# A two-block transformer kernel: two of five gate-and-up chunks per feed-forward as seven block products

## The chip, the cores and the metric

The kernel runs on one core of a Trainium2 chip. The metric is the device time of one execution in microseconds (us); the kernel before takes 1632.77 us, the median of three runs. Names of engines are those of the profile: PE is TensorE (matmuls; PEld are its weight loads), DVE is VectorE, ACT is ScalarE, POOL is GpSimd, SP is SyncE, whose queue issues the DMAs.

## The reference, cut to what matters

256 rows of 1024 elements pass through two blocks, all in float32. Block 1 has two gated feed-forwards, a mixer and a gated side input. Block 2 has four feed-forwards (called s0 to s3 below), a gated linear attention between s0 and s1 and a retention between s2 and s3, each followed by a layer norm. The four feed-forwards are:

```python
def swiglu_2(x, w_in, w_out):            # x 256x1024, w_in 1024x5632, w_out 2816x1024
    gate, up = jnp.split(x @ w_in, 2, axis=-1)
    return (jax.nn.silu(gate) * up) @ w_out
...
        h = layer_norm(DN_ALPHA * h + 0.5 * swiglu_2(h, ffn_w_in[i, 0], ffn_w_out[i, 0]), ln_g[i, 0], ln_b[i, 0])
```

## The kernel before, in words

**Units.** Weights come from memory in units of 128x2048 float32 (1 MB each). A unit is half of the 1024-deep contraction (four blocks of 128 rows) for 512 columns. `fetch` (lines 145 to 163) loads one into a `raw` tile by an SP DMA, rounds it on ACT to `whi` (line 159) and lets DVE write what is left over, `wlo = raw - whi` (line 162). There are 4 `raw` tiles and 5 each of `whi` and `wlo`. Activations, transposed, are split in the same manner (`split`, lines 193 to 200). So each float32 block product is three matmuls of 128x512 (`mm3`, lines 179 to 183: hi·hi, hi·lo, lo·hi).

**A feed-forward** (`ffn`, lines 344 to 399). The 256 rows are two tiles, t = 0 and 1. The 2816 hidden columns are five chunks (c = 0 to 4) of 512 columns of gate and of up, and a last one of 256 and 256. A chunk has four units: gate lower half, gate upper half, up lower half, up upper half. For each t and each of gate and up the PE adds 8 blocks into one PSUM tile (`mm`, 5 of them), which makes 2 x 2 x 8 x 3 = 96 matmuls a chunk. `finish` (line 348) then takes silu of gate on ACT (`sg`, line 352) and multiplies by up on DVE (`pr`, line 353). `turn` transposes both `pr` tiles on PE (4 + 4 transposes of 128x128, line 190) and splits them into `hT`, input of the down product (`lagged`, lines 304 to 342, 11 units).

**What sets the order.** The code is written in one sequence. `unit` (line 165) hands out the next unit of the plan (`all_units`, line 68) and fetches further ones ahead; `defer` and `tick` put steps such as transposes some matmuls later. A scheduler then gives every engine its own order; on the chip every queue goes in order, and semaphores join them. At the end of a layer `ln_post` (line 264) writes y, and `turn_in` (line 249) transposes it for the next one.

Of the kernel before, what the change touches and what calls it, by code (L numbers as in the profile page):

```python
# [11 lines left out]
F32 = mybir.dt.float32  # L12
F32R = mybir.dt.float32r
# [6 lines left out]
P = 128  # L20
# [29 lines left out]

def ffn_units(g, u, d):

    out = []
    for c in range(5):
        out += [(g, 2 * c), (g, 2 * c + 1), (u, 2 * c), (u, 2 * c + 1)]
    return out + [(g, 10), (g, 11)] + [(d, i) for i in range(11)]
# [4 lines left out]


MIX_ORDER = [1, 0, 2, 3, 4, 5, 6, 7]
GLA_ORDER = [1, 0, 2, 4, 3, 5]
# [15 lines left out]

class Build:
# [6 lines left out]
    def open(self, ctx):  # L88
        def pool(name, space=None):
# [55 lines left out]
    def fetch(self, fine=False, begun=None):  # L145

        nc = self.nc
        name, i = self.plan[len(self.ready)]
        raw = begun or self.T("raw", [P, UNIT], F32)
        hi = self.T("whi", [P, UNIT], F32R)  # L150
        lo = self.T("wlo", [P, UNIT], F32R)
        parts = 4 if fine else 1
        n = UNIT // parts
        for j in range(parts):
            s = slice(j * n, (j + 1) * n)
            if begun is None or j:
# [57 lines left out]
    def sumsq(self, srcs, scale):  # L214

        st = self.small(len(srcs), "ss")
        for i, s in enumerate(srcs):
            jk = self.T("jk", [P, CW], F32)
            self.nc.scalar.activation(jk[:, :s.shape[-1]], s, AF.Square, scale=scale, accum_out=st[:, i:i + 1])  # L219
        return st  # L220
# [27 lines left out]

    def turn_in(self, xT, t, n, u):

        self.defer(TURN[t] + n, lambda: xT.__setitem__(n, self.splitT(u)))

# [10 lines left out]

    def ln_post(self, t, acc, g, b, half, last=False):

# [15 lines left out]
        for n in range(2):  # L281
            sl = slice(n * CW, (n + 1) * CW)
            y = self.T("y", [P, CW], F32)
            nc.vector.scalar_tensor_tensor(out=y, in0=h[:, sl], scalar=r, in1=b[:, sl], op0=ALU.mult, op1=ALU.add)  # L284
            if last:
                nc.sync.dma_start(out=self.out[t * P:(t + 1) * P, sl], in_=y)
            else:
                self.turn_in(xT, t, n, y)
                self.nc.gpsimd.tensor_scalar(out=h[:, sl], in0=y, scalar1=ALPHA, scalar2=0.0, op0=ALU.mult, op1=ALU.add)
# [3 lines left out]
    def proj(self, ps, x, w, n=CW, kb=4, k0=0, nk=None):  # L293


        nk = nk or kb * len(w)
        for i in range(kb * len(w)):
            k = k0 + i
            self.settle(lambda: x[k // 4] is not None)
            self.mm3(ps[:, :n], x[k // 4][:, k % 4, :], w[i // kb][:, i % kb, :n], k == 0, k == nk - 1)  # L300
            if i % 2:
                self.tick()

    def lagged(self, x, name, n_units, after, lag=LAG, have=None, extra=None):
# [38 lines left out]

    def ffn(self, xT, r, wg, wu, wd, after, first=False):
        nc = self.nc
        hT = {}

        def finish(c, t, ps_g, ps_u, n):
# [41 lines left out]
        for t in range(0 if first else 1, NT):  # L390
            finish(0, t, pss[t, wg], pss[t, wu], CW)
        for c in range(1, 6):
            for nm in (wg, wu) if c < 5 else (wg,):
                w = [self.unit(nm, 2 * c + i, 4) for i in range(2)]
                for t in range(NT):
                    pss[t, nm] = self.M()
                    self.proj(pss[t, nm], xT[t], w)
# [218 lines left out]
    def gla(self, xT, after):  # L616
# [235 lines left out]
    def run(self, ctx):  # L852
# [12 lines left out]
        nc.scalar.activation(warm, self.mhalf[:, :1], AF.Silu)  # L865
        idle = self.T("jk", [P, CW], F32).bitcast(BF16)[:, :CW]
        nc.gpsimd.memset(idle, 0.0)
# [58 lines left out]
        def ln_layer(body, i, half, last):  # L926
            g, b = self.gain("gp", f"ln_g{i}"), self.gain("gq", f"ln_b{i}")
            xT = [None] * NT

            def after(t, acc):  # L930
                xT[t] = self.ln_post(t, acc, g, b, half, last)

# [3 lines left out]
        for i in range(6):  # L936
            if i % 3 != 1:
                f = 2 * (i // 3) + (i % 3) // 2
                body = lambda after: self.ffn(nx, None, f"s{f}g", f"s{f}u", f"s{f}d", after)
# [4 lines left out]
            nx = ln_layer(body, i, i % 3 != 1, i == 5)  # L944

# [110 lines left out]
```

## Time and profile before

| | |
|---|---|
| time, median of 3 runs | 1632.77 us (1632.32 to 1633.8) |
| the profiled execution, its own time | 1633.42 us |
| its span, first to last instruction | 1631.6 us |
| granted PE clock, mean over the span | 0.997 of full speed (2.4 GHz) |
| PE busy | 1619.3 us (99%), 7520 matmul records |
| DVE busy | 932.8 us (57%) |
| ACT busy | 722.3 us (44%) |
| POOL busy | 131.3 us (8%) |
| DMA | 308 MB, mean 189 GB/s |

Busy time is the union of the spans of an engine's instructions. Matmuls overlap each other in the pipeline, so the time that one of them costs is read from the distance between the starts of two that follow each other, not from its own span. The same holds for two DVE or ACT instructions that stand one behind the other. Idle time of an engine costs nothing unless another engine waits at its end.

### The profile page before, as it was taken

Reading aid. Unit: us, or ns where it says so; the run is one execution under the profiler, and the core shown is the slowest. Engines: PE = TensorE matmul, PEld = TensorE weight load, DVE = VectorE, ACT = ScalarE, POOL = GpSimd, SP = SyncE. Lnnn points to the kernel's source line nnn. Section 1 sums busy time; section 2 is a strip of 40 time slices with the busy share of each in tenths; the row PEclk is TensorE's granted clock in tenths of the full one; section 3 lists DMA queues with packets and bytes.
Section 4 is the critical chain, followed back from the end, with each engine's and each line's share of the span. In section 5 each row is a group of like instructions: output and inputs, shape, how many; then the busy total and the mean of one; then the engine's idle time right before and its main releaser. Section 6 shows DMA issues by size and latency. Waiting matters only on the chain. (4 is left out here: it accounts for less than half of the span.)

```text
span 1631.6 us, 18183 instructions
## 1 busy us (share of the span) xinstructions
PE 1619.3 (99%) x7520; PEld 1339.6 (82%) x7520; DVE 932.8 (57%) x818; ACT 722.3 (44%) x715; POOL 131.3 (8%) x138
## 2 busy tenths in 40 slices
PE   9999999999999999999999999999999999999998
PEld 6888888888888888888888888888887888888886
DVE  5644665575543865446747544664538666485444
ACT  6443555444433744433644443444424444344431
POOL 0000200020000300003012000100003300010000
PEclk9999999999999999999999999999999999999999
DMA  9754664545454664545536454555445644464540
GB/s 357 262 189 155 221 218 143 205 175 213 167 194 155 226 227 163 201 155 207 195 135 225 168 200 155 195 219 206 173 162 206 216 155 160 149 238 176 204 146 35
DMA packets 49650, 308.09 MB, mean 189 GB/s; under 512 B 6032, under 2 KB 7056, under 8 KB 14880
## 3 DMA queue, kind: packets, MB, share of 16 engines
q1 hardware_dynamic: 49280, 306.67, 51.6%
q8 instruction: 59, 0.97, 0.2%
q10 hardware_dynamic: 288, 0.27, 0.1%
q14 instruction: 23, 0.19, 0.0%
HBM read 305.86 MB, written 1.05 MB: 188 GB/s over the span
## 5 line engine op out<-in xcount | busy, mean ns | idle before, releaser
L162 DVE TENSOR_TENSOR wlo<-raw,whi 128x2048 fp32r<-128x2048 f32 (+1 forms) x287 | 631.4, 2206 | 480.6 <-ACT whi L159 480.5
L159 ACT CAST whi<-raw 128x2048 fp32r<-128x2048 f32 (+1 forms) x286 | 524.1, 1838 | 554.6 <-PE mm L183 190.2
L181 PE MATMUL mm<-whi,xTh 128*128 128x512 f32 x1296 | 514.0, 397 | 0.0
L183 PE MATMUL mm<-whi,xTl 128*128 128x512 f32 x1296 | 505.8, 390 | 0.4 <-DVE xTl L199 0.4
L182 PE MATMUL mm<-wlo,xTh 128*128 128x512 f32 x1296 | 504.6, 389 | 0.0
L183 PEld LDWEIGHTS mm<-whi,xTl 128*128 128x128 f32 x1296 | 243.2, 188 | 52.9 <-DVE xTl L199 1.2
L181 PEld LDWEIGHTS mm<-whi,xTh 128*128 128x128 f32 x1296 | 243.4, 188 | 49.7 <-issue 1.7
L182 PEld LDWEIGHTS mm<-wlo,xTh 128*128 128x128 f32 x1296 | 243.7, 188 | 48.0
L181 PE MATMUL acc<-whi,hTh 128*128 128x512 f32 x528 | 207.0, 392 | 0.0
L183 PE MATMUL acc<-whi,hTl 128*128 128x512 f32 x528 | 205.7, 389 | 0.0
L182 PE MATMUL acc<-wlo,hTh 128*128 128x512 f32 x528 | 205.5, 389 | 0.0
L183 PEld LDWEIGHTS acc<-whi,hTl 128*128 128x128 f32 x528 | 99.1, 188 | 20.9
L181 PEld LDWEIGHTS acc<-whi,hTh 128*128 128x128 f32 x528 | 99.1, 188 | 20.1
L182 PEld LDWEIGHTS acc<-wlo,hTh 128*128 128x128 f32 x528 | 99.2, 188 | 20.0
L199 DVE TENSOR_TENSOR hTl<-hT,hTh 128x512 fp32r<-128x512 f32 (+1 forms) x72 | 43.7, 642 | 61.0 <-ACT hTh L198 61.0
L276 POOL TENSOR_TENSOR rl<-mv,mhalf 128x1 f32<-128x1 f32 x12 | 11.8, 984 | 762.1 <-DVE mv L275 762.1
L181 PE MATMUL mm<-whi,xh 128*128 128x512 f32 x176 | 69.4, 397 | 1.8 <-ACT xh L884 1.3
L182 PE MATMUL mm<-wlo,xh 128*128 128x512 f32 x176 | 69.2, 393 | 0.2 <-DVE wlo L162 0.2
L183 PE MATMUL mm<-whi,xl 128*128 128x512 f32 x176 | 69.3, 394 | 0.0
L225 POOL TENSOR_TENSOR v<-ss 128x1 f32<-128x1 f32 x16 | 25.1, 1567 | 522.6 <-ACT jk L219 522.6
L352 ACT ACTIVATE sg<-mm 128x512 f32<-128x512 f32 (+1 forms) x48 | 26.9, 560 | 87.3 <-PE mm L183 87.3
L198 ACT CAST hTh<-hT 128x512 fp32r<-128x512 f32 (+1 forms) x72 | 36.6, 554 | 26.3 <-PE hT L190 26.3
(219 smaller groups left out, 1242.4 us busy)
## 6 DMA issues: line engine op xcount, KB each, us to landing
raw<-in_rin SPq DMA_DIRECT2D x24, 1024.0 KB, 4.8
raw<-in_bin SPq DMA_DIRECT2D x16, 1024.0 KB, 5.1
raw<-in_f2g SPq DMA_DIRECT2D x12, 1024.0 KB, 4.8
raw<-in_s0g SPq DMA_DIRECT2D x12, 1024.0 KB, 4.8
raw<-in_gin SPq DMA_DIRECT2D x12, 1024.0 KB, 4.8
raw<-in_s1g SPq DMA_DIRECT2D x12, 1024.0 KB, 4.8
raw<-in_s2g SPq DMA_DIRECT2D x12, 1024.0 KB, 4.8
raw<-in_s3g SPq DMA_DIRECT2D x12, 1024.0 KB, 4.8
```

The source lines that it names most:

```text
L159: nc.scalar.copy(hi[:, s], raw[:, s])
L162: nc.vector.tensor_tensor(out=lo[:, s], in0=raw[:, s], in1=hi[:, s].bitcast(F32), op=ALU.subtract)
L181: mm(ps, x.hi, w.hi, start=start, stop=False)
L182: mm(ps, x.hi, w.lo, start=False, stop=False)
L183: mm(ps, x.lo, w.hi, start=False, stop=stop)
L198: self.nc.scalar.copy(hi, v)
L199: self.nc.vector.tensor_tensor(out=lo, in0=v, in1=hi.bitcast(F32), op=ALU.subtract)
L225: self.nc.gpsimd.tensor_tensor(out=v, in0=st[:, 0:1], in1=st[:, 1:2], op=ALU.add)
L276: nc.gpsimd.tensor_tensor(out=r, in0=mv[:, 1:2], in1=self.mhalf[:, :1], op=ALU.pow)
L352: nc.scalar.activation(sg[:, :n], ps_g[:, :n], AF.Silu)
```

## The change

In each of the four feed-forwards of block 2, chunks 2 and 4 are computed in another way. A chunk is the product of a 2x2 block matrix (row tiles t by halves of the contraction) with a 2x2 block matrix (halves of the contraction by gate and up). Instead of eight block products it is now made of seven, over sums of blocks (`seven`). The weight sums `a+b`, `b+c`, `a+b+c` and `a+b+c+d` are made by DVE in the raw tiles, in place (`fetch_sum`); each of the seven operands is then split into `whi` and `wlo`. The sums of activations (`y`) are made once per feed-forward from copies of the transposed tiles (`turn_in`, `sums_in`). The results are put together by DVE (`seven`). The other chunks now take a unit at a time over both row tiles, in block 1 too. There are 5 `raw` tiles instead of 4; two small tiles change place or type (`jk`, `wg`).

```diff
+SUMS = (("a", None), ("a", "b"), ("b", "c"), ("a", "c"), ("c", None), ("d", None), ("a", "d"))
...
+        four = [(g, 2 * c), (g, 2 * c + 1), (u, 2 * c), (u, 2 * c + 1)]
+        out += [(four, j) for j in range(7)] if c in seven else four
...
+SEVEN = (2, 4)
...
-    BUFS = {"raw": 4, "whi": 5, "wlo": 5, "S": 28, "mm": 5, "tp": 3, "y": 2, "u": 2,
+    BUFS = {"raw": 5, "whi": 5, "wlo": 5, "S": 28, "mm": 5, "tp": 3, "y": 2, "u": 2,
...
+    def fetch_sum(self, four, j):
...
+        for key, at in {0: (("a", 0), ("b", 2)), 2: (("c", 3),), 5: (("d", 1),)}.get(j, ()):
+            r[key] = self.T("raw", [P, UNIT], F32)
+            nc.sync.dma_start(out=r[key], in_=self.ins[four[at][0]][four[at][1]])
+        key, other = SUMS[j]
+        if other:
+            nc.vector.tensor_tensor(out=r[key], in0=r[key], in1=r[other], op=ALU.add)
+        hi, lo = self.T("whi", [P, UNIT], F32R), self.T("wlo", [P, UNIT], F32R)
+        nc.scalar.copy(hi, r[key])
+        nc.vector.tensor_tensor(out=lo, in0=r[key], in1=hi.bitcast(F32), op=ALU.subtract)
+        return Split(hi, lo)
...
+    def sums_in(self, raws):
...
+        sub(r2, r2, raws[1])
+        sub(r4, r4, r2)
...
+            self.nc.scalar.copy(hi, v)
+            self.nc.vector.tensor_tensor(out=lo, in0=v, in1=hi.bitcast(F32), op=ALU.subtract)
...
+    def seven(self, x, y, four, done):
...
+        def times(name, x, j):
+            ps = self.M(name)
+            w = self.unit(four, j, 4, 4)
+            for k in range(4):
+                self.mm3(ps, x[:, k, :], w[:, k, :], k == 0, k == 3)
...
+        nc.scalar.copy(p1, times("P1", x[0][0], 0))
+        p5 = times("P5", y[1], 1)
+        p7 = times("P7", y[3], 2)
+        TT(out=u2, in0=times("P6", y[2], 3), in1=p1, op=ALU.subtract)
+        TT(out=u4, in0=p5, in1=u2, op=ALU.add)
+        TT(out=c22, in0=u4, in1=p7, op=ALU.subtract)
+        TT(out=u2, in0=u2, in1=p7, op=ALU.subtract)
+        TT(out=u4, in0=times("P3", y[4], 4), in1=u4, op=ALU.add)
+        TT(out=p1, in0=times("P2", x[0][1], 5), in1=p1, op=ALU.add)
+        done(0, p1, u4)
+        TT(out=u2, in0=times("P4", x[1][1], 6), in1=u2, op=ALU.subtract)
+        done(1, u2, c22)
...
         for c in range(1, 6):
+            if raws is not None and c == 1:
+                self.defer(4, lambda: y.update(self.sums_in(raws)))
+            if raws is not None and c in SEVEN:
+                self.settle(lambda: y)
+                self.seven(xT, y, [(wg, 2 * c), (wg, 2 * c + 1), (wu, 2 * c), (wu, 2 * c + 1)], finish7(c))
+                continue
             for nm in (wg, wu) if c < 5 else (wg,):
-                w = [self.unit(nm, 2 * c + i, 4) for i in range(2)]
+                for i in range(2):
+                    w = [self.unit(nm, 2 * c + i, 4, 3 if raws is not None else 2)]
+                    for t in range(NT):
+                        if i == 0:
+                            pss[t, nm] = self.M()
+                        self.proj(pss[t, nm], xT[t], w, CW, 4, 4 * i, KD)
```

How it moves the instructions is shown at three places. In the names below, a number behind a tile tells its instances apart, and the L numbers of the changed kernel are those of its own file.

The first is DVE's queue in s0 up to the first seven-product chunk. Of the kernel before, from the last part of one ordinary chunk to the next:

```order
L353 TENSOR_TENSOR pr_4632<-mm_4606,sg_4631 128x512
L162 TENSOR_TENSOR wlo_4746<-raw_4744,whi_4745 128x2048
L353 TENSOR_TENSOR pr_4661<-mm_4635,sg_4660 128x512
L162 TENSOR_TENSOR wlo_4752<-raw_4750,whi_4751 128x2048
L199 TENSOR_TENSOR hTl_4712<-hT_4701,hTh_4711 128x512
L199 TENSOR_TENSOR hTl_4716<-hT_4706,hTh_4715 128x512
L162 TENSOR_TENSOR wlo_4816<-raw_4814,whi_4815 128x2048
L162 TENSOR_TENSOR wlo_4822<-raw_4820,whi_4821 128x2048
```

and of the change, the lead-in to chunk 2 (L186 is the subtraction of a sum's unit, L183 the addition of two raw tiles; the first `wlo` is that of P1, the next that of P5):

```order
L186 TENSOR_TENSOR wlo_4458<-raw_4453,whi_4457 128x2048
L183 TENSOR_TENSOR raw_4453<-raw_4453,raw_4455 128x2048
L223 TENSOR_TENSOR hTl_4432<-hT_4426,hTh_4431 128x512
L304 TENSOR_TENSOR yTl_4442<-y3_4296,yTh_4441 128x512
L183 TENSOR_TENSOR raw_4455<-raw_4455,raw_4516 128x2048
L304 TENSOR_TENSOR yTl_4450<-xr_4169,yTh_4449 128x512
L186 TENSOR_TENSOR wlo_4487<-raw_4453,whi_4486 128x2048
L183 TENSOR_TENSOR raw_4453<-raw_4453,raw_4516 128x2048
```

Where four large subtractions stood in a chunk, there are now additions between them, each ahead of the cast and subtraction of the same tile.

The second is DVE's queue behind chunk 2's last subtraction of a weight sum (the four large rows are units of the ordinary chunk 3):

```order
L168 TENSOR_TENSOR wlo_4640<-raw_4638,whi_4639 128x2048
L223 TENSOR_TENSOR hTl_4616<-hT_4606,hTh_4615 128x512
L378 TENSOR_TENSOR u2_4556<-P6_4637,p1_4555 128x512
L168 TENSOR_TENSOR wlo_4663<-raw_4661,whi_4662 128x2048
L379 TENSOR_TENSOR u4_4557<-P5_4582,u2_4556 128x512
L168 TENSOR_TENSOR wlo_4683<-raw_4681,whi_4682 128x2048
L380 TENSOR_TENSOR c22_4558<-u4_4557,P7_4619 128x512
L381 TENSOR_TENSOR u2_4556<-u2_4556,P7_4619 128x512
L382 TENSOR_TENSOR u4_4557<-P3_4660,u4_4557 128x512
L383 TENSOR_TENSOR p1_4555<-P2_4680,p1_4555 128x512
L168 TENSOR_TENSOR wlo_4707<-raw_4705,whi_4706 128x2048
L455 TENSOR_TENSOR pr_4701<-u4_4557,sg_4700 128x512
```

The chunk's `pr` stands behind all of them, where before it came straight behind the chunk's last matmul.

The third is PE's queue at the transposes of a chunk's `pr`. Before, both stand together:

```order
L183 MATMUL mm_4526<-whi_4515,xTl_4164 128x512
L190 MATMUL hT_4551<-ident_212,pr_4482 128x128 x4
L190 MATMUL hT_4556<-ident_212,pr_4511 128x128 x4
L181 MATMUL mm_4569<-whi_4451,xTh_4286 128x512
L182 MATMUL mm_4569<-wlo_4452,xTh_4286 128x512
```

and now, 24 matmuls behind the last of the seven products, the first of two:

```order
L207 MATMUL mm_4741<-whi_4639,xTl_4291 128x512
L214 MATMUL hT_4754<-ident_212,pr_4701 128x128 x4
L205 MATMUL mm_4728<-whi_4662,xTh_4165 128x512
L206 MATMUL mm_4728<-wlo_4663,xTh_4165 128x512
L207 MATMUL mm_4728<-whi_4662,xTl_4166 128x512
```

The second, `hT_4759<-pr_4725`, stands 13 matmuls further on; both stop the queue until DVE has written their `pr`.

## Rows read from the trace of the kernel before

**Rows 1.** The page, part 1: busy time, share of span, instructions of each engine.
```profile
PE 1619.3 (99%) x7520; PEld 1339.6 (82%) x7520; DVE 932.8 (57%) x818; ACT 722.3 (44%) x715; POOL 131.3 (8%) x138
```
**Rows 2.** Waits of PE, all of the span: us in total, times, longest us.
```profile
PE mm L181 <- ACT xh L884: 1.3, 1, 1.3
PE spin L870 <- POOL jk L867: 1.3, 1, 1.3
PE xT L190 <- DVE y L284: 1.0, 1, 1.0
PE mm L183 <- DVE xTl L199: 0.4, 1, 0.4
PE mm L181 <- ACT whi L159: 0.4, 1, 0.4
PE mm L182 <- DVE wlo L162: 0.2, 1, 0.2
```
**Rows 3.** Busy time by stretch: two stretches of one chunk's length, s0, chunks 1 to 3.
```profile
core 0: us, PE busy (x) PEld busy (x) DVE busy (x) ACT busy (x) POOL busy (x), PEclk, DMA share, GB/s
...
609.30:631.95 22.65, 22.65 (x106) 18.85 (x105) 11.66 (x9) 9.69 (x8) 0.00 (x0) 1.00 0.50 184
631.95:654.60 22.65, 22.65 (x106) 18.81 (x105) 11.62 (x9) 9.69 (x8) 0.00 (x0) 1.00 0.50 186
```
**Rows 4.** PE in order of time, s0: start us, us, instruction.
```profile
618.76 0.39 PE L182 MATMUL mm<-wlo,xTh 128*128 128x512 f32 x1
618.99 0.39 PE L183 MATMUL mm<-whi,xTl 128*128 128x512 f32 x1
619.21 0.39 PE L181 MATMUL mm<-whi,xTh 128*128 128x512 f32 x1
619.44 0.39 PE L182 MATMUL mm<-wlo,xTh 128*128 128x512 f32 x1
619.66 0.39 PE L183 MATMUL mm<-whi,xTl 128*128 128x512 f32 x1
619.90 1.03 PE L190 MATMUL hT<-ident,pr 128*128 128x128 f32 x8
620.69 0.48 PE L181 MATMUL mm<-whi,xTh 128*128 128x512 f32 x1
621.00 0.40 PE L182 MATMUL mm<-wlo,xTh 128*128 128x512 f32 x1
```
**Rows 5.** Groups, shapes apart: busy us, mean ns | idle before.
```profile
L162 DVE TENSOR_TENSOR wlo<-raw,whi 128x2048 fp32r<-128x2048 f32 x271 | 621.4, 2296 | 480.4 <-ACT whi L159 480.3
L159 ACT CAST whi<-raw 128x2048 fp32r<-128x2048 f32 x271 | 515.9, 1906 | 554.6 <-PE mm L183 190.2 <-issue 182.1 <-PE acc L183 165.7
L199 DVE TENSOR_TENSOR hTl<-hT,hTh 128x512 fp32r<-128x512 f32 x60 | 39.2, 687 | 51.9 <-ACT hTh L198 51.8
L262 DVE TENSOR_TENSOR h<-h,y 128x512 f32<-128x512 f32 x16 | 10.3, 684 | 0.0
```
**Rows 6.** DVE in order of time, s0, chunks 1 and 2; idle before in brackets.
```profile
613.91 2.29 DVE L162 TENSOR_TENSOR wlo<-raw,whi 128x2048 fp32r<-128x2048 f32 x1 [4.01 <-ACT whi L159]
616.12 0.68 DVE L353 TENSOR_TENSOR pr<-mm,sg 128x512 f32<-128x512 f32 x1
616.72 2.28 DVE L162 TENSOR_TENSOR wlo<-raw,whi 128x2048 fp32r<-128x2048 f32 x1
```
**Rows 7.** The loads of s0's gate units.
```profile
DMA to landing us min/median/max: 4.7/4.8/6.6
```
**Rows 8.** POOL in order of time, in the retention.
```profile
1256.19 0.74 POOL L793 TENSOR_TENSOR rot<-rb,ra 128x256 f32<-128x256 f32 x1
1261.78 2.65 POOL L792 TENSOR_TENSOR rot<-ra,rb 128x256 f32<-128x256 f32 x1 [4.85 <-DVE rb L789]
```
**Rows 9.** DVE in order of time, the same stretch.
```profile
1258.14 2.29 DVE L162 TENSOR_TENSOR wlo<-raw,whi 128x2048 fp32r<-128x2048 f32 x1 [2.80 <-ACT whi L159]
...
1261.55 5.03 DVE L162 TENSOR_TENSOR wlo<-raw,whi 128x2048 fp32r<-128x2048 f32 x2
```

More of the change, by code (lines that the diff above doesn't have):

```diff
@@ L48, in __getitem__, with ffn_units @@
         return Split(self.hi[i], self.lo[i])
-def ffn_units(g, u, d):
+def ffn_units(g, u, d, seven=()):
     out = []
     for c in range(5):
-        out += [(g, 2 * c), (g, 2 * c + 1), (u, 2 * c), (u, 2 * c + 1)]
+        four = [(g, 2 * c), (g, 2 * c + 1), (u, 2 * c), (u, 2 * c + 1)]
+        out += [(four, j) for j in range(7)] if c in seven else four
     return out + [(g, 10), (g, 11)] + [(d, i) for i in range(11)]
@@ L148, in fetch @@
         name, i = self.plan[len(self.ready)]
+        if isinstance(name, list):
+            return self.ready.append(self.fetch_sum(name, i))
         raw = begun or self.T("raw", [P, UNIT], F32)
@@ L163, in fetch @@
         self.ready.append(Split(hi, lo))
+    def fetch_sum(self, four, j):
+        nc = self.nc
+        if j == 0:
+            self.sums = {}
+        r = self.sums
+        for key, at in {0: (("a", 0), ("b", 2)), 2: (("c", 3),), 5: (("d", 1),)}.get(j, ()):
[8 more added lines that the diff above has]
+        return Split(hi, lo)
     def unit(self, name, i, kb, ahead=1):
@@ L247, in rms_in, with turn_in, turn @@
         return xT, self.row_rstd(t)
-    def turn_in(self, xT, t, n, u):
-        self.defer(TURN[t] + n, lambda: xT.__setitem__(n, self.splitT(u)))
+    def turn_in(self, xT, t, n, u, raws=None):
+        def turn():
+            ps = self.transpose4(u, 4, "xT")
+            xT[n] = self.split(ps, 4, "xT")
+            if raws is None:
+                return
+            if (t, n) != (1, 1):
+                raws[t, n] = self.S([P, CW], name="xr")
+                self.nc.scalar.copy(raws[t, n], ps)
+            if (t, n) == (1, 0):
+                raws[3] = self.S([P, CW], name="y3")
+                self.nc.vector.tensor_tensor(out=raws[3], in0=raws[0, 0], in1=ps, op=ALU.subtract)
+            if (t, n) == (1, 1):
+                raws[1] = raws.pop((1, 0))
+                self.nc.vector.tensor_tensor(out=raws[1], in0=raws[1], in1=ps, op=ALU.subtract)
+        self.defer(TURN[t] + n, turn)
+    def sums_in(self, raws):
+        sub = lambda o, a, b: self.nc.vector.tensor_tensor(out=o, in0=a, in1=b, op=ALU.subtract)
+        r2, r4 = raws.pop((0, 0)), raws.pop((0, 1))
+        sub(r2, r2, raws[1])
+        sub(r4, r4, r2)
+        y = {}
+        for i, r in ((1, raws.pop(1)), (3, raws.pop(3)), (2, r2), (4, r4)):
+            tile = (lambda n: self.T("ld", [P, CW], F32R, name=n).rearrange("p (a b) -> p a b", a=4)) if i < 3 else \
+                (lambda n: self.S([P, 4, P], F32R, n))
+            hi, lo, v = tile("yTh"), tile("yTl"), r.rearrange("p (a b) -> p a b", a=4)
+            self.nc.scalar.copy(hi, v)
+            self.nc.vector.tensor_tensor(out=lo, in0=v, in1=hi.bitcast(F32), op=ALU.subtract)
+            y[i] = Split(hi, lo)
+        return y
     def rms_post(self, t, acc, gpost, half):
@@ L262, in rms_post, with ln_post @@
             nc.vector.tensor_tensor(out=h[:, sl], in0=h[:, sl], in1=y, op=ALU.add)
-    def ln_post(self, t, acc, g, b, half, last=False):
+    def ln_post(self, t, acc, g, b, half, last=False, raws=None):
         nc, h = self.nc, self.h[t]
@@ L342, in lagged, with ffn @@
         after(1, acc[1])
-    def ffn(self, xT, r, wg, wu, wd, after, first=False):
+    def ffn(self, xT, r, wg, wu, wd, after, first=False, raws=None):
         nc = self.nc
@@ L362, in finish, with finish7, done @@
                 self.defer(4, lambda: hT.__setitem__((t, c), self.splitT(pr, n // P, "hT")))
+        def finish7(c):
+            prs = []
+            def done(t, a, b):
+                sg = self.T("sg", [P, CW], F32)
+                pr = self.T("sg", [P, CW], F32, name="pr")
+                nc.scalar.activation(sg, a, AF.Silu)
+                nc.vector.tensor_tensor(out=pr, in0=b, in1=sg, op=ALU.mult)
+                prs.append(pr)
+                if t:
+                    self.defer(4, lambda: turn(c, CW, *prs))
+            return done
         first_pr = {}
@@ L865, in run @@
         nc.scalar.activation(warm, self.mhalf[:, :1], AF.Silu)
-        idle = self.T("jk", [P, CW], F32).bitcast(BF16)[:, :CW]
+        idle = self.T("jk", [P, CW], BF16)
         nc.gpsimd.memset(idle, 0.0)
@@ L930, in after @@
             def after(t, acc):
-                xT[t] = self.ln_post(t, acc, g, b, half, last)
+                xT[t] = self.ln_post(t, acc, g, b, half, last, raws)
             body(after)
@@ L943, in run @@
                 body = lambda after: self.ret(nx, after)
-            nx = ln_layer(body, i, i % 3 != 1, i == 5)
+            sums = {} if i in (1, 2, 4) else None
+            nx = ln_layer(body, i, i % 3 != 1, i == 5, sums)
+            raws = sums
 def units(w, kb, n):
```

30 lines of the change are left out of this document (17 added, 13 removed).

## The prediction

> **What bounds the kernel now.** I first read the page's busy shares: PE is busy 99% of the span, DVE 57%, ACT 44% [rows 1]. A busy share alone does not make PE the bound, since a PE that waits between short pieces can look busy. So I read PE's own waits next. In 1631.6 us there are six kinds with 4.6 us together, and 2.6 of them are at the very start [rows 2]. No load, cast or subtraction holds PE anywhere in the feed-forwards. The third view is the order of time on PE: matmuls of 128x512 start 0.22 to 0.23 us apart (618.76 to 619.66 is four steps), and eight transposes with the longer step behind them take 619.90 to 621.00, 1.10 us, of which 0.23 is the matmul's own step: 0.87 us [rows 4]. A stretch of one chunk's length, 96 matmuls and eight transposes, takes 22.65 us at full granted clock [rows 3]; without the 0.87 that is 21.78, or 0.227 us a matmul. So a chunk lasts what its matmuls last. In the same stretch DVE is busy 11.7 us and ACT 9.7: DVE has 11 us to spare in an ordinary chunk.
>
> **The change part by part.**
>
> *Removed.* A chunk of seven products has 7 x 4 x 3 = 84 matmuls instead of 96. Two chunks in four feed-forwards: 8 x 12 = 96 matmuls fewer. At the step of 0.227 us [rows 3, 4] that is **21.8 us**. The Trainium skill, TensorE: Matmul & The Clock Gate, section Back-to-back issue gap, gives about 131 ns for a 512-column matmul in a sustained stream. By that figure the estimate would be 96 x 0.131 = 12.6 us saved and 1620.8 us in all; the trace does not agree, since its steps are 0.227 us in these very stretches [rows 4], and the sum goes by them.
>
> *Added on DVE and ACT, weights.* Four loads stay four. But seven units are cast and split instead of four, and four additions come in. A large DVE subtraction lasts 2.30 us alone and is 2.21 apart from the next instruction (613.91 to 616.12), a small one 0.69 and 0.60 apart (616.12 to 616.72) [rows 5, 6]. No large float32 addition in place is in the trace; the nearest row is the small one, `h<-h,y`, with 684 ns against 687 for the small subtraction [rows 5], so I take 2.21 us for it. Bounds: 2.21 below, and above what a subtraction beside POOL costs, 5.03 - 2.29 = 2.74 us [rows 9]. A seven-product chunk asks of DVE 11 large instructions (24.3 us) and 6 sums of products, 2 `pr` and 2 `hTl` (10 x 0.60 = 6.0): 30.3 us, against 84 x 0.227 + 0.87 = 19.9 us of PE. Alone it would be bound by DVE by 10.4 us. Its ordinary neighbour has 4 large and 4 small, 11.2 us, against 22.65. **As a pair: DVE 41.5 us, PE 42.6 us.** So DVE goes from about half busy to nearly full, and all depends on whether it may work ahead.
>
> *How far ahead it may work.* Five `whi` and `wlo` tiles: four units may lie ready while one is multiplied. I walked the three queues from the start of chunk 1 of s0, in the order of the change, with the steps above, 1.91 us for a cast [rows 5] and 4.8 us for a load [rows 7]. When PE reaches P1 at 22.2 us, DVE has done the subtractions of P1, P5, P7 and P6 (the last at 21.0) and three of the four additions. One hop as an example: P3 takes the tile of chunk 1's last unit, free at 22.2; its cast ends at 24.1; DVE, done with P6's step at 20.9, does `pr`, the addition a+d, `pr` (20.9 + 0.60 + 2.25 + 0.60 = 24.35) and then P3's subtraction until 26.6. PE needs it at 34.0. The others, ready against needed: P2 29.6 and 36.7, P4 31.9 and 39.4, chunk 3's first unit 35.5 and 42.2, chunk 4's P6 67.7 and 73.9, its P4 77.2 and 82.1, and the last chunk's first unit 80.1 and 84.8. **The shortest lead is 4.7 us**, so the weights cost PE nothing.
>
> *Raw tiles.* The tile of `a` lives from P1 to P4. With five, the load behind a chunk's four takes the tile of `b`, which P7's subtraction lets go at 17.5 us, not that of `a` at 31.9; it lands 4.8 us later, at 22.3, for a cast at 34. Hidden.
>
> *Sums of activations.* Per feed-forward 7 small ACT copies and casts and 8 small DVE instructions, 4.8 us of DVE in chunks 0 and 1, where the leads are 10 us and more. They stand behind the first `xT` splits, so the stage's own start keeps its lead but for one copy of 0.50 us between two splits that PE uses 12 matmuls apart. Nothing.
>
> *Transposes of `pr`.* Here the lead is thin. From P7's end (31.2) DVE's queue runs: wait for a cast until 33.2, then four large steps, one `hTl`, six sums of products and the first `pr`: 33.2 + 4 x 2.21 + 7 x 0.60 + 0.69 = 46.9. PE comes to the transposes six groups of 12 matmuls behind P7: 31.2 + 16.3 = 47.5, or 47.4 with the walk's own times. Lead about 0.4 us; the second transposes have 0.4 as well, where the kernel before has 3.5. There are two such places in each of 8 chunks, and a PSUM tile of the last chunk, let go by a sum of products, has the same 0.4 us: 20 places. Bounds for one: 0, and 0.6 us if that chain of 13.7 us runs 7% longer. I take 0.04 each, 0.8 us in all, near the lower end, since steps of one kind repeat to 0.02 us [rows 6].
>
> *Other chunks and block 1.* The same 96 matmuls, a unit at a time over both row tiles; the other PSUM tiles are let go at least 1.1 us before use by the same walk. Nothing, either sign.
>
> **Sum.** On the profiled execution: 1633.42 - 21.8 + 0.8 = 1612.4 us. That execution is 0.65 us above the median shown, so the forecast for the median is **1611.8 us**, 1.3% less.
>
> **The rivals.**
>
> (a) *The thin places wait.* If DVE's chains or ACT's casts run 5% longer than the walk, each place comes some 13.7 x 0.05 - 0.4 = 0.3 us late, and 20 x 0.3 = 6 us go; at the upper bound 20 x 0.6 = 12 us. On 1611.0, without the 0.8: 1617 to 1623. For it: 0.4 us is little, and both engines now run side by side without rest. Against: steps repeat closely [rows 6]. Chance 0.16.
>
> (b) *DVE becomes the bound: slower.* Mechanism: large subtractions and additions at 2.74 us, as the one that ran beside POOL [rows 9], while POOL's own instruction took 2.65 instead of 0.74 us [rows 8]. Place: the pairs of chunks 1 to 4. Price: a pair has 15 large ones, so 15 x 0.53 = 8.0 us more: 49.5 us of DVE against 42.6 of PE, 6.9 late per pair, 13.8 per feed-forward. The lead of 4.7 us pays part; 9.1 us remain, four times is 36: 1647 us. It decides from the point where a large instruction exceeds 2.21 + (2 x 1.1 + 4.7) / 30 = 2.44 us; at 2.62 the whole gain is eaten. Against: POOL is idle in these stretches (0.00 in both) [rows 3], and its two `h` instructions per row tile stay ahead of chunk 1, where leads are long. The Trainium skill, SBUF — State Buffer, section Who interferes with whom, states that a DVE instruction with two SBUF inputs and a GpSimd instruction that reads SBUF exclude each other, and the trace agrees (2.65 against 0.74 us) [rows 8]; the additions are of that kind, so any POOL work that slips in would be paid. Chance 0.04.
>
> (c) *The raw tiles run short: no gain or slower.* If the load behind a chunk had to wait for the tile of `a` (31.9 us), it would land at 36.7, its cast end at 38.6, and the sums of products queued behind that subtraction would come 2.5 to 5 us late, with PSUM tiles that P4 needs. 8 x 2.5 to 5 is 20 to 40 us: 1631 to 1651. Against: the load waits for `b`'s last reader. Chance 0.04.
>
> (d) *PE still executes as many matmuls* (a fill-in, another step per product): within 0.2% of before. The order shows 96 fewer, of the same shape. Chance 0.02.
>
> **How the numbers follow.** The forecast, with the thin places at 0 to 0.2 us each (1611.0 to 1615), has 0.74. A difference under 0.2%, 3.3 us, is about what a measurement of this kernel can't tell from none. Forecast and (a) are both faster: 0.74 + 0.16 = 0.90, and I give 0.01 of (c) to it: 0.91. Same: (d) and 0.02 of (c), 0.04. Slower: (b) and 0.01 of (c), 0.05. The range reaches from 1609.8 (all of the 21.8 us, and 1.2 for the spread of executions) to 1620.0, into (a) but short of its upper bound; it leaves out half of (a) and all of (b), (c) and (d), some 0.18.
>
> **What would show it.** Right: PE's 128x512 matmuls 96 fewer with steps still 0.227 us; a seven-product chunk of about 19.9 us; DVE busy near 932.8 + 8 x (30.3 - 11.2) + 4 x 4.8, about 1105 us, with PE's waits still a few us. Wrong: waits of PE on `wlo` inside chunks 2 to 5 (b or c), on `pr` at the transposes (a), or large DVE additions well over 2.3 us each.

## The result, and the profile after

| | before | after |
|---|---|---|
| time, median | 1633.28 us (4 runs beside the change) | **1612.4 us** (1611.83 to 1613.37, 4 runs) |
| ratio, 95% interval | | 0.9875 [0.9862, 0.9887] |
| span of the profiled execution | 1631.6 us | 1610.3 us |
| granted PE clock, mean | 0.997 | 0.999 |

The kernel became 1.25% faster. The forecast was 1611.8 us with a range of 1609.8 to 1620.0: it held, and the likeliest case was the right one.

The page's first part, of the kernel after (answers to [rows 1]):

```profile
PE 1598.0 (99%) x7424; PEld 1320.8 (82%) x7424; DVE 1103.8 (69%) x962; ACT 786.5 (49%) x775; POOL 129.6 (8%) x138
```

PE has 96 matmuls fewer and is busy 21.3 us less; the span of the profiled execution is 21.3 us shorter, and the medians differ by 20.9 us. DVE is busy 1103.8 us, 171 more, where the prediction had about 1105. So PE gave back just its own removed work, and nothing of DVE's 171 us came through.

PE's waits after, the whole span: us in total, times, longest (answers to [rows 2]):

```profile
PE mm L205 <- ACT xh L991: 1.4, 1, 1.4
PE spin L977 <- POOL jk L974: 1.3, 1, 1.3
PE xT L214 <- DVE y L339: 1.0, 1, 1.0
PE xT L214 <- DVE h L317: 0.5, 1, 0.5
PE mm L207 <- DVE xTl L223: 0.4, 1, 0.4
```

4.6 us again, as before. No `wlo`, `whi`, `pr` or tile of a sum stands here: none of the new chunks makes PE wait. The only new row is 0.5 us on `h` at 578.42, where block 2 begins; e1, without any seven products, has it as well.

Busy time of one seven-product chunk, s0's chunk 4, from its first matmul to the next chunk's first, columns as in [rows 3]:

```profile
657.04:676.99 19.95, 19.95 (x94) 16.59 (x93) 19.70 (x13) 14.83 (x10) 0.00 (x0) 1.00 0.64 232
```

The chunk lasts the 19.9 us that were forecast. DVE is busy 19.70 of 19.95 us: it is as full as PE here, and PE does not wait.

DVE's and ACT's groups after, shapes apart (answers to [rows 5]; L183 is the addition in place, L185 and L186 cast and subtraction of a unit of the seven products):

```profile
L168 DVE TENSOR_TENSOR wlo<-raw,whi 128x2048 fp32r<-128x2048 f32 x239 | 547.8, 2295 | 356.1 <-ACT whi L165 356.1
L186 DVE TENSOR_TENSOR wlo<-raw,whi 128x2048 fp32r<-128x2048 f32 x56 | 127.1, 2285 | 4.5 <-ACT whi L185 4.5
L183 DVE TENSOR_TENSOR raw<-raw 128x2048 f32<-128x2048 f32 x32 | 73.1, 2285 | 0.2
...
L185 ACT CAST whi<-raw 128x2048 fp32r<-128x2048 f32 x56 | 107.0, 1910 | 71.0 <-DVE raw L183 39.0
```

The large addition, which the trace before did not have, lasts 2285 ns like the subtraction. The cast keeps its time (1910 ns, 1906 before). Before an ordinary subtraction DVE idles 1.49 us on the mean (356.1 over 239), before one of the seven products 0.08 (4.5 over 56). That says the same as the window: where the seven products are, DVE goes on nearly without a break.

The thin places, at the transposes of chunk 2's `pr` in s0. DVE in order of time (idle before in brackets):

```profile
638.59 0.68 DVE L455 TENSOR_TENSOR pr<-u,sg 128x512 f32<-128x512 f32 x1
639.20 0.68 DVE L385 TENSOR_TENSOR u<-P,u 128x512 f32<-128x512 f32 x1
639.80 2.28 DVE L186 TENSOR_TENSOR wlo<-raw,whi 128x2048 fp32r<-128x2048 f32 x1
642.00 0.69 DVE L455 TENSOR_TENSOR pr<-c,sg 128x512 f32<-128x512 f32 x1
```

and PE, which needs them:

```profile
639.51 0.40 PE L207 MATMUL mm<-whi,xTl 128*128 128x512 f32 x1
639.74 0.60 PE L214 MATMUL hT<-ident,pr 128*128 128x128 f32 x4
640.10 0.48 PE L205 MATMUL mm<-whi,xTh 128*128 128x512 f32 x1
...
643.16 0.60 PE L214 MATMUL hT<-ident,pr 128*128 128x128 f32 x4
```

The first `pr` ends at 639.27 and PE takes it at 639.74; the second ends at 642.69 and PE takes it at 643.16. The lead is 0.47 us both times (0.4 was forecast), and it held.

### The profile page after: what moved, and what is told of

Read it like the earlier page. It is cut to its first block, busy times and chain, and to the rows that moved or that the text cites. A ratio compares the mean times of both kernels' runs of the same rounds, so it can differ in the third digit from the quotient of the medians.

```text
span 1610.3 us, 18239 instructions
## 1 busy us (share of the span) xinstructions
PE 1598.0 (99%) x7424; PEld 1320.8 (82%) x7424; DVE 1103.8 (69%) x962; ACT 786.5 (49%) x775; POOL 129.6 (8%) x138
## 5 line engine op out<-in xcount | busy, mean ns | idle before, releaser
L168 DVE TENSOR_TENSOR wlo<-raw,whi 128x2048 fp32r<-128x2048 f32 (+1 forms) x255 | 557.9, 2194 | 356.3 <-ACT whi L165 356.2
L165 ACT CAST whi<-raw 128x2048 fp32r<-128x2048 f32 (+1 forms) x254 | 463.0, 1830 | 431.8 <-PE acc L207 195.1
L205 PE MATMUL mm<-whi,xTh 128*128 128x512 f32 x1040 | 413.8, 398 | 0.0
L207 PE MATMUL mm<-whi,xTl 128*128 128x512 f32 x1040 | 406.1, 391 | 0.4 <-DVE xTl L223 0.4
L206 PE MATMUL mm<-wlo,xTh 128*128 128x512 f32 x1040 | 405.9, 390 | 0.0
L207 PEld LDWEIGHTS mm<-whi,xTl 128*128 128x128 f32 x1040 | 195.2, 188 | 42.8 <-DVE xTl L223 1.1
L206 PEld LDWEIGHTS mm<-wlo,xTh 128*128 128x128 f32 x1040 | 195.6, 188 | 38.1
L185 ACT CAST whi<-raw 128x2048 fp32r<-128x2048 f32 x56 | 107.0, 1910 | 71.0 <-DVE raw L183 39.0
L186 DVE TENSOR_TENSOR wlo<-raw,whi 128x2048 fp32r<-128x2048 f32 x56 | 127.1, 2285 | 4.5 <-ACT whi L185 4.5
L207 PEld LDWEIGHTS acc<-whi,hTl 128*128 128x128 f32 x528 | 99.1, 188 | 20.9
L183 DVE TENSOR_TENSOR raw<-raw 128x2048 f32<-128x2048 f32 x32 | 73.1, 2285 | 0.2
```

The costliest lines, as they stand in the source:

```text
L183: nc.vector.tensor_tensor(out=r[key], in0=r[key], in1=r[other], op=ALU.add)
L185: nc.scalar.copy(hi, r[key])
L186: nc.vector.tensor_tensor(out=lo, in0=r[key], in1=hi.bitcast(F32), op=ALU.subtract)
L205: mm(ps, x.hi, w.hi, start=start, stop=False)
L206: mm(ps, x.hi, w.lo, start=False, stop=False)
L207: mm(ps, x.lo, w.hi, start=False, stop=stop)
```

## The experiments

The theory (A in the expectations) is the prediction's: the gain is the 96 matmuls, the rest of the change is neutral, and DVE's work hides as long as a pair of chunks and the lead cover it. What it says of DVE can fail in three ways: by DVE's sum, by the place where its instructions fall, and by the tiles. All kernels are the change with one alteration, in one table (spans and busy times of the profiled execution; the idle time of PE is span less busy):

| kernel | time, us | ratio to before [95%] | span | PE busy | PE idle | DVE busy | clock |
|---|---|---|---|---|---|---|---|
| after | 1612.4 | 0.9875 [0.9862, 0.9887] | 1610.3 | 1598.0 | 12.3 | 1103.8 | 0.999 |
| e1, none | 1634.11 | 1.0006 [0.9996, 1.0016] | 1630.9 | 1618.0 | 12.9 | 953.1 | 0.999 |
| e2, only 4 | 1623.84 | 0.9943 [0.9928, 0.9957] | 1621.4 | 1609.2 | 12.2 | 1029.5 | 0.999 |
| e3, 2 and 3 | 1648.6 | 1.0097 [1.0082, 1.0112] | 1646.7 | 1612.3 | 34.4 | 1106.4 | 0.993 |
| e4, four raw | 1612.63 | 0.9874 [0.9859, 0.9889] | 1611.7 | 1598.6 | 13.1 | 1103.7 | 0.997 |
| e5, one extra at P1 | 1621.99 | 0.9928 [0.9913, 0.9943] | 1619.4 | 1601.4 | 18.0 | 1121.8 | 0.998 |
| e6, four extra | 1683.35 | 1.0307 [1.029, 1.0325] | 1680.2 | 1629.7 | 50.5 | 1175.7 | 0.983 |
| e7, additions on POOL | 1662.81 | 1.0178 [1.0163, 1.0194] | 1660.9 | 1615.9 | 45.0 | 1104.6 | 0.989 |
| e8, block 1 too | 1607.4 | 0.9839 [0.9825, 0.9854] | 1605.4 | 1592.3 | 13.1 | 1146.2 | 0.998 |
| e9, one extra at P7 | 1612.17 | 0.9872 [0.9857, 0.9886] | 1610.4 | 1598.2 | 12.2 | 1121.0 | 0.999 |
| e10, two extra at P7 | 1635.05 | 1.0013 [1.0004, 1.0023] | 1634.9 | 1609.2 | 25.7 | 1139.7 | 0.994 |
| e11, 1 and 3 | 1644.44 | 1.0069 [1.0054, 1.0084] | 1642.6 | 1611.9 | 30.7 | 1105.0 | 0.996 |

### e1: all of the change but the seven products

```diff
-SEVEN = (2, 4)
+SEVEN = ()
```

> No chunk is made of seven products; the fifth raw tile, the loop that takes a unit at a time and the earlier fetches stay. Theory A (the gain is the 96 matmuls at 0.227 us, all else is covered): back to the kernel before, 1632 to 1634 us, ratio 1.000 to it. Theory B (part of the gain comes from the fifth raw tile or from the other order of the ordinary chunks): clearly under it, 1615 to 1629 us.

Measured: 1634.11 us, 1.0006 [0.9996, 1.0016]. The unit-by-unit order of the ordinary chunks, the sums of activations, the fifth raw tile and the moved small tiles together change nothing that can be measured (the time lies 0.1 us over the range expected). All of the gain stands in the seven products.

### e2: half of them

```diff
-SEVEN = (2, 4)
+SEVEN = (4,)
```

> Chunk 4 alone is made of seven products. Theory A: half the matmuls are gone, 48 x 0.227 = 10.9 us, so 1632.8 - 10.9 = 1621.9, within 1621 to 1623.5. Theory B: the second seven-product chunk runs with VectorE nearly full and gives less than the first, so that one alone is worth more than half of the 20.9 us measured: 1618 to 1620.5.

Measured: 1623.84 us. With chunk 4 alone 10.3 us are gained on e1's time, with chunk 2 added another 11.4. The two halves are equal within what a run varies, and each is near 48 x 0.227 = 10.9 us. The time lies a little over the range expected; the two chunks add up, so neither takes from the other.

### e3: the same seven products, in neighbouring chunks

```diff
-SEVEN = (2, 4)
+SEVEN = (2, 3)
```

> Chunks 2 and 3 instead of 2 and 4: the same 96 matmuls fewer, but no ordinary chunk between them. Theory A (VectorE must be paid for by an ordinary neighbour): two neighbours ask 60.6 us of VectorE against 39.8 of TensorE, 20.8 over; the lead that is there at the first one's end (some 7 us) and the ordinary chunk behind don't cover it, 6 to 8 us late in each feed-forward: 1636 to 1645 us, slower than the kernel before. Rival (the count of matmuls alone decides): 1612 us.

Measured: 1648.6 us, 36 more than the change with the same 7424 matmuls, and 15 slower than the kernel before. The loss is in the direction that the balance gives and larger than the range. PE's waits in it, as above:

```profile
PE P L206 <- DVE wlo L186: 9.5, 7, 1.8
PE mm L205 <- ACT whi L165: 4.9, 5, 1.3
PE P L205 <- ACT whi L185: 4.1, 5, 1.6
PE hT L214 <- DVE pr L455: 2.8, 4, 0.7
```

and the stretch of s0 where the second of the two chunks is multiplied, columns as in [rows 3]:

```profile
640.00:660.00 20.00, 13.99 (x61) 10.21 (x59) 19.16 (x16) 11.94 (x11) 0.00 (x0) 0.99 0.55 191
660.00:680.00 20.00, 19.98 (x85) 16.41 (x86) 19.02 (x16) 13.73 (x11) 0.00 (x0) 0.92 0.90 329
```

DVE is full (19.16 of 20) and PE has 13.99 us of work: without an ordinary chunk ahead, the chunk is bound by DVE. In the next stretch PE hardly stands still, yet does 85 matmul records, where 20 us at full clock hold some 94 (the row of the whole chunk above), at a granted clock of 0.92. So PE loses time again after its waits are over; more of this at e10.

### e4: four raw tiles

```diff
-    BUFS = {"raw": 5, "whi": 5, "wlo": 5, "S": 28, "mm": 5, "tp": 3, "y": 2, "u": 2,
+    BUFS = {"raw": 4, "whi": 5, "wlo": 5, "S": 28, "mm": 5, "tp": 3, "y": 2, "u": 2,
```

> Four raw tiles instead of five, all else as in the change. Theory A (a load waits for the tile of b, c or d, let go 5 us and more before it is needed, and the tile of a is not in the way): same time, 1611.5 to 1613.5 us. Rival (the fifth tile carries the change; with four a load waits for the tile that lives through all seven products): 2.5 us and more lost in each of 8 chunks, 1630 us or more.

Measured: 1612.63 us, the change's time. The fifth raw tile is not needed, and rival (c), loads that run short of raw tiles, falls even with a tile less than the change has.

### e5: one extra large subtraction per seven-product chunk, at the first product

It writes the same `wlo` a second time (`j` is the number of the product, in the order P1, P5, P7, P6, P3, P2, P4).

```diff
         nc.vector.tensor_tensor(out=lo, in0=r[key], in1=hi.bitcast(F32), op=ALU.subtract)
+        if j == 0:
+            nc.vector.tensor_tensor(out=lo, in0=r[key], in1=hi.bitcast(F32), op=ALU.subtract)
```

> In each seven-product chunk the subtraction of the first unit is done twice (same operands, same result): one large VectorE instruction more in each, 2.21 us. Theory A by its balance of pairs: 43.7 us of VectorE against 42.6, 1.1 late a pair and 2.2 a feed-forward, under the lead of 4.7: no more than 2 us lost, 1612 to 1614.5. Rival (the thin places and the order of the queues decide, not the balance): each is moved by up to the extra instruction's 2.2 us, some 2 us lost in each feed-forward: 1619 to 1623.

Measured: 1621.99 us, 9.6 more than the change and within the rival's range. The balance (DVE 43.7 us a pair against 42.6, less the lead) had said next to nothing; it fails here. PE in order of time at the end of s0's chunk 4, in the product P4:

```profile
674.11 0.39 PE L209 MATMUL P<-whi,xTl 128*128 128x512 f32 x1
674.58 0.51 PE L207 MATMUL P<-whi,xTh 128*128 128x512 f32 x1
676.38 0.50 PE L207 MATMUL mm<-whi,xTh 128*128 128x512 f32 x1 [1.29 <-ACT whi L165]
676.91 0.50 PE L208 MATMUL P<-wlo,xTh 128*128 128x512 f32 x1
677.25 0.40 PE L209 MATMUL P<-whi,xTl 128*128 128x512 f32 x1
```

The first matmul of P4 (674.58) starts 0.47 instead of 0.23 us behind the one before, since its cast ends only at 674.53. Behind it stands a matmul of the next chunk (`mm`), which in the change comes only after P4, and the profile puts the wait down to that matmul's cast. But P4's own second matmul (676.91) reads the `wlo` that DVE has written at 676.85, as the rows below show. So the `mm` stands in a gap that P4 would have had without it; what is late is P4's own unit. From 674.11 to 677.25 there are four steps, 0.91 us by 0.227, and they take 3.14: 2.2 us lost, four times 8.9 of the 9.1 us between the two spans. The cause of the late unit is on DVE, in the same chunk:

```profile
657.37 0.69 DVE L439 TENSOR_TENSOR pr<-mm,sg 128x512 f32<-128x512 f32 x1 [1.19 <-PE mm L209]
657.98 2.28 DVE L183 TENSOR_TENSOR raw<-raw 128x2048 f32<-128x2048 f32 x1
662.44 6.70 DVE L186 TENSOR_TENSOR wlo<-raw,whi 128x2048 fp32r<-128x2048 f32 x3 [2.18 <-ACT whi L185]
...
670.25 2.28 DVE L183 TENSOR_TENSOR raw<-raw 128x2048 f32<-128x2048 f32 x1
...
674.56 2.29 DVE L186 TENSOR_TENSOR wlo<-raw,whi 128x2048 fp32r<-128x2048 f32 x1
```

against the change:

```profile
652.61 2.29 DVE L183 TENSOR_TENSOR raw<-raw 128x2048 f32<-128x2048 f32 x1
...
657.29 0.69 DVE L437 TENSOR_TENSOR pr<-mm,sg 128x512 f32<-128x512 f32 x1 [1.80 <-PE mm L207]
...
662.30 2.29 DVE L183 TENSOR_TENSOR raw<-raw 128x2048 f32<-128x2048 f32 x1
```

The third addition comes 5.4 us later: besides the extra instruction, it now stands behind both `pr` of chunk 3, of which the second waits 1.19 us for PE, where in the change it stands ahead of them. The cast behind it comes later too, DVE now idles 2.18 us for that cast, and the last addition, P4's, comes 8 us later; its cast and its subtraction (674.56) can only follow. One extra instruction of 2.2 us became 8, because additions, casts and subtractions form a chain over two engines, and the queue's order around them changed as well.

### e6: four extra

```diff
+        if other:
+            nc.vector.tensor_tensor(out=lo, in0=r[key], in1=hi.bitcast(F32), op=ALU.subtract)
```

> In each seven-product chunk the subtractions of the four units that are sums are done twice: four large VectorE instructions more, 8.8 us. Theory A: a pair asks 50.3 us of VectorE against 42.6 of TensorE, 7.7 late a pair, 15.4 a feed-forward, of which the lead pays 4.7: 4 x 10.7 = 43 us lost, 1648 to 1664 us. Rival (VectorE has more cover than the walk gives it): 1612 to 1625.

Measured: 1683.35 us, 71 more than the change and beyond the range expected. PE's two largest waits:

```profile
PE mm L208 <- DVE wlo L168: 23.6, 8, 3.9
PE P L207 <- ACT whi L185: 10.4, 8, 1.3
```

DVE is the bound now, as the balance says, but the price is higher: by it (7.7 us late per pair, twice, less 4.7, four times) it should be 43 us. PE idles 38.2 us more than in the change, near the balance's figure. The other 31.7 us are PE's own busy time, for the same matmuls: the mean granted clock is 0.983.

### e7: the additions on GpSimd

```diff
-            nc.vector.tensor_tensor(out=r[key], in0=r[key], in1=r[other], op=ALU.add)
+            nc.gpsimd.tensor_tensor(out=r[key], in0=r[key], in1=r[other], op=ALU.add)
```

> The four additions of weights in each seven-product chunk go to GpSimd. A GpSimd instruction of 128x256 takes 0.74 us alone, so 128x2048 some 5.9. Theory A (a GpSimd instruction and a VectorE one with two operands in SBUF shut each other out, as the 2.65 us beside 0.74 suggest): VectorE's 7 large and its small ones, 15.5 + 6.0, and 23.6 of GpSimd add up to 45.1 us a chunk and 56.3 a pair against 42.6 of TensorE; 13.7 late a pair, some 20 us a feed-forward: 1670 to 1710. Rival (they run side by side): VectorE gets 8.8 us a chunk free, TensorE stays the bound, 1611 to 1616.

Measured: 1662.81 us, between the two, near the first. The instructions on `raw`, with the shortest, median and longest ns:

```profile
L186 DVE TENSOR_TENSOR wlo<-raw,whi x56: 2272/2282/6685, 594.7 to 1569.7; 128x2048 fp32r<-128x2048 f32 x56
L183 POOL TENSOR_TENSOR raw<-raw x32: 4546/4627/6589, 597.1 to 1560.9; 128x2048 f32<-128x2048 f32 x32
```

An addition takes 4627 ns on POOL at the median, against 2285 on DVE. Of the 56 subtractions, the 34 that overlap no addition keep their time (2.27 to 2.29 us). Of the 22 that do, 18 last 4.87 to 6.69 us; the other four began just before an addition and keep 2.28 us, and in those four cases the addition takes 6.59 us. So the one that begins later waits for the other, as theory A has it. DVE's busy time, in which such a wait counts, is the change's (1104.6 and 1103.8 us): what is taken off DVE comes back as the time that its other instructions take, with a longer chain besides.

### e8: block 1's second feed-forward as well

```diff
-    p += ffn_units("f2g", "f2u", "f2d")
+    p += ffn_units("f2g", "f2u", "f2d", SEVEN)
...
-                nc.vector.tensor_tensor(out=pr, in0=b, in1=sg, op=ALU.mult)
+                    nc.vector.scalar_tensor_tensor(out=pr, in0=b, scalar=r[t], in1=sg, op0=ALU.mult, op1=ALU.mult)
```

(with `sums_in` and `seven` called there as in block 2).

> Chunks 2 and 4 of the second feed-forward of block 1 are made of seven products as well (the row scale stays in the silu and in the multiplication behind it). Theory A: 24 matmuls fewer, 5.4 us, covered like the others: 1612.4 - 5.4 = 1607.0, within 1606 to 1609. Rival (block 1's feed-forward, whose last steps on VectorE are a little longer, has no cover left): 1609 to 1618.

Measured: 1607.4 us (1606.42 to 1608.02), 0.9839 [0.9825, 0.9854]: **faster than both kernels**. 24 matmuls fewer are 5.4 us, and 5.0 came. PE's waits stay few: six, 5.4 us together, the longest 1.8, and none on a unit of the new chunks.

### e9: e5's extra subtraction, at the third product

```diff
+        if j == 2:
+            nc.vector.tensor_tensor(out=lo, in0=r[key], in1=hi.bitcast(F32), op=ALU.subtract)
```

> The same one extra large subtraction (2.2 to 2.3 us of DVE) in each seven-product chunk as in the run that put it at the first product and lost 9.6 us, now at the third product, P7, where the queues as traced leave DVE waiting. Place theory (a loss comes from where DVE's instruction falls, and from the order that the scheduler then writes for PE, not from DVE's sum): 1611.5 to 1614.5 us, PE's waits a few us as in the changed kernel. Rival, DVE's sum: the pair of chunks already uses up its slack and lead, so 2.2 us more per chunk costs the same wherever it stands: 1619 to 1624 us.

Measured: 1612.17 us, the change's time, with DVE 17 us busier. The same instruction that cost 9.6 us at P1 costs nothing at P7. DVE in s0's chunk 4:

```profile
652.78 2.28 DVE L183 TENSOR_TENSOR raw<-raw 128x2048 f32<-128x2048 f32 x1
654.98 2.28 DVE L188 TENSOR_TENSOR wlo<-raw,whi 128x2048 fp32r<-128x2048 f32 x1
657.18 0.68 DVE L439 TENSOR_TENSOR pr<-mm,sg 128x512 f32<-128x512 f32 x1
```

The third addition is where the change has it (652.78 and 652.61). The extra one (L188) falls into the 1.80 us in which DVE waits for PE in the change, in the rows shown with e5. So at one extra instruction a pair DVE's sum does not decide; the place does, and the order that comes with it.

### e10: two of them, at the third product

```diff
+        for _ in range(2 if j == 2 else 0):
+            nc.vector.tensor_tensor(out=lo, in0=r[key], in1=hi.bitcast(F32), op=ALU.subtract)
```

> Two extra large subtractions at the third product in each seven-product chunk: DVE 45.9 us per pair of chunks against 42.6 of PE, 3.3 late per pair, less the lead of 4.7 us once per feed-forward. The prediction's balance: (2 x 3.3 - 4.7) x 4 = 7.6 us more, 1620 us. With the order and tile releases as traced (a walk of the queues with traced durations): about 1630 us. Rival, no bound on DVE near here: 1612 to 1614.

Measured: 1635.05 us (1631.96 to 1637.18 over ten runs; the profiled one took 1636.67): the second extra costs 22.9 us, the change's whole gain, where the balance has 7.6; the walk, about 1630, was nearer. PE in order of time, s0, chunk 4:

```profile
676.48 0.39 PE L209 MATMUL P<-whi,xTl 128*128 128x512 f32 x1
677.46 0.50 PE L207 MATMUL P<-whi,xTh 128*128 128x512 f32 x1 [0.59 <-ACT whi L185]
679.26 0.73 PE L207 MATMUL mm<-whi,xTh 128*128 128x512 f32 x2 [1.29 <-ACT whi L165]
...
681.00 0.63 PE L208 MATMUL P<-wlo,xTh 128*128 128x512 f32 x1
681.42 0.63 PE L209 MATMUL P<-whi,xTl 128*128 128x512 f32 x1
...
684.07 0.39 PE L208 MATMUL mm<-wlo,xTh 128*128 128x512 f32 x1
```

P4's subtraction on DVE:

```profile
677.52 2.28 DVE L186 TENSOR_TENSOR wlo<-raw,whi 128x2048 fp32r<-128x2048 f32 x1
```

and the stretches around it, columns as in [rows 3]:

```profile
676.00:680.00 4.00, 2.11 (x8) 1.01 (x7) 3.80 (x5) 4.00 (x3) 0.00 (x0) 1.00 0.85 303
680.00:684.00 4.00, 4.00 (x11) 3.14 (x12) 4.00 (x4) 4.00 (x4) 0.00 (x0) 0.57 0.81 291
684.00:688.00 4.00, 4.00 (x20) 3.29 (x19) 4.00 (x3) 2.95 (x2) 0.00 (x0) 1.00 0.92 342
```

PE is busy 2.11 us of the first four. As in e5, matmuls of the next chunk (`mm`) stand in the gap, and P4's second matmul starts at 679.85, as its `wlo` is ready at 679.80. In the four us behind it PE waits for nothing, but the granted clock is 0.57, most of the time its lower level of 1.2 GHz: steps are 0.42 us (681.00 to 681.42) instead of 0.23, and 11 records fit in where 20 do afterwards. From 676.48 to 684.07 there are 15 steps, 3.4 us by 0.227; they take 7.6, and 4.2 us are lost, where the waits shown come to 1.9. Earlier in the same chunk P6's unit is late too: from 666.61 to 669.20 there are three steps, 0.7 us, and they take 2.6. The 4.2 and 1.9 us make up the loss of this feed-forward (24.6 us between the spans, a quarter is 6.1). The ten runs go with the clock: the quickest has a mean granted clock of 0.997, the slowest 0.993. In s0 all three waits of PE on units stand in chunk 4 and none in chunk 2: the first pair still finds its lead, the second does not.

### e11: chunks 1 and 3

```diff
-SEVEN = (2, 4)
+SEVEN = (1, 3)
```

> Seven products in chunks 1 and 3 instead of 2 and 4: the same 96 matmuls fewer, and still an ordinary chunk ahead of each and behind each. Pair balance alone: 1611 to 1614 us. Rival, the lead must have been built by then: chunk 1 follows a chunk 0 that begins with an empty lead, since the layer norm's work and the sums of activations stand in DVE's queue there, so waits of PE on whi and wlo in chunk 1, four times 3 to 6 us: 1625 to 1640 us.

Measured: 1644.44 us, 32 more than the change and above the rival's range. Each chunk has an ordinary one before it and behind it, so the balance of pairs is the change's; what differs is where the first of them begins, one chunk into the stage. PE's largest waits:

```profile
PE mm L205 <- ACT whi L165: 9.9, 8, 1.3
PE xT L214 <- DVE y L339: 3.4, 3, 1.2
PE P L205 <- ACT whi L185: 2.7, 3, 0.9
```

Eight on the first unit behind a seven-product chunk, one in every chunk of that kind: the place within P4 again. Three wait for the layer norm's `y`, where the change has one of 1.0 us. In s0, where chunk 1 is multiplied:

```profile
600.00:620.00 20.00, 17.48 (x67) 13.20 (x67) 19.42 (x14) 14.48 (x11) 0.00 (x0) 0.91 0.53 195
```

DVE is full (19.42 of 20), PE does 67 records where the full clock gives 94, at a granted 0.91. The rival, a lead not yet built, is borne out in direction; how much of it the sums of activations make, which this kernel needs a chunk earlier, was not tried. That chunk 3 waits as well fits with a stage that has been late since chunk 1, but was not tried apart.

## Why the prediction was right, point by point

- **What bounds.** Right. PE's removed work came out of the span one for one: 21.3 us of busy time, 21.3 of span, 20.9 between the medians, forecast 21.8. e2 and e8 repeat it, with 48 and 24 matmuls. The steps that [rows 4] show are still 0.227 us (19.95 less 0.87 us over 84 matmuls), and with 7424 records rival (d) fell. The sum by the 131 ns of the Trainium skill (TensorE: Matmul & The Clock Gate, section Back-to-back issue gap), 1620.8 us, lies 8 us off; the measurement decides.
- **The price of an unseen operation.** Right. The large addition, taken at 2.21 us between 2.21 and 2.74, lasts 2285 ns on the mean like the subtraction, and the next instruction starts 2.20 us behind it (643.20 to 645.40).
- **DVE's count.** Wrong by one: `seven` has seven sums of products, not six (e1 has 112 DVE instructions fewer than the change, 14 a chunk: seven large and seven small). A seven-product chunk asks 30.9 us of DVE and not 30.3, the pair 42.1 against 42.6. The lead still covers it, so the forecast stood. But the slack was half of what was written, and that the total came out at 1103.8 us against about 1105 is in part luck: with the seventh sum it is about 1110.
- **The lead.** Right, within 0.2 us in the place checked: the prediction's walk has chunk 4's P4 ready 4.9 us early. In the trace the subtractions of that chunk's last two units begin at 664.51 and 667.31 (2.28 us long). P4 starts at 674.27, 4.7 us behind the end of its subtraction, and the first matmul that reads its `wlo` at 674.49, 4.9 us behind.
- **Raw tiles, sums of activations, other chunks: nothing.** Right: e4 needs one raw tile less, e1 shows the rest at 1.0006 [0.9996, 1.0016]. That the fifth tile was what let the load go ahead, as the step on raw tiles implied, is not so: four do as well.
- **Thin places.** Their lead was right (0.47 us, forecast 0.4); the 0.8 us taken for them were not lost, since no `pr` wait is among PE's. Rival (a) fell. That the net gain of 21.0 us forecast came out to 0.1 us (20.9 between the medians) is luck in part: the 0.8 us taken here stand in for the 0.9 by which the medians' difference falls short of 21.8, which is within what the runs vary.
- **Rival (b), DVE as the bound.** Its deciding point was near for the better placement. It was given as 2.44 us per large instruction, which is 3.4 us more of DVE per pair (2.40 and 2.9 with the seventh sum); e9 (2.2 more) loses nothing and e10 (4.4 more) does. Its *price* behind the point was wrong: "9.1 remain per feed-forward" counts a late microsecond once. e10 lost 22.9 us where that reckoning has 7.6, e6 71 where it has 43, and the whole gain was gone at 4.4 us more per pair, not at the 6.1 that 2.62 us per instruction stand for. With the seventh sum the reckoning gives 12.4 for e10 and 47.6 for e6; PE's idle time rose by 13.4 and 38.2. What it leaves out altogether is that PE's steps are longer after it has waited: PE's busy time rises by 0.55 to 0.84 us for each us more of idle time, in e3, e5, e6, e7, e10 and e11 alike. Part of that is the granted clock, as at e10; in e5 the clock stays at 1.00 around the wait (674 to 678 and 678 to 682), and the two steps behind it are 0.53 and 0.34 us all the same.
- **"As a pair."** Too generous as a rule, though it came out right here. e5 has the sum of e9 and loses 9.6 us; e11 has the pairs of the change and loses 32. What the prediction rested on was the walk of the queues from the start of the stage, with chunk 2 as the first; the pair's sum alone would have allowed both.

What stays open: why the scheduler wrote another order around the additions in e5, and how much of the 8 us is due to that order and how much to the extra instruction itself, was not tried. Nor is it shown how PE's longer steps divide between the clock and the rest in e3, e6, e7 and e11.

## What to carry to other kernels

When work moves from a full engine to a half-empty one, check three things apart: the sum over the stretch that the buffers span, the lead at the place where it begins, and the slot in the other queue where each instruction falls; here the same 2.2 us were free at one product and cost 9.6 us at another. Where the sum is near its bound, price a microsecond of PE's waiting above one; in the six kernels here it came to 1.55 to 1.84. Before a wait is put down to the instruction that stands in the queue there, look when the operand of the next one was ready. And put such chunks where the stage has already built a lead, with an ordinary one between.

## What the runs showed that was not expected

- After PE stood about 1.9 us of four, the granted clock of the next four was 0.57 in e10, with steps of 0.42 us; then it was back at 1.00. Over e6 the mean is 0.983, and PE is busy 31.7 us longer for the same 7424 matmuls.
- A 128x2048 float32 addition takes 4.63 us on GpSimd (median of 32), about twice DVE's 2.285. A DVE subtraction of the same size that begins while one runs lasts 4.87 to 6.69 us instead of 2.28, and the rest keep their time. So DVE's busy time fell by none of the 73.1 us that were taken off it.
